# A rotary embedding on one core: another order of loads on SyncE, another branch in the load and store helpers, and a row of small loads

## The chip, the cores and the metric

The kernel runs on one core of one Trainium2 chip. The metric is the device time of one execution in microseconds (us). Three runs of the kernel before gave 316.74 to 316.91 us, with a median of 316.77 us.

Four engines and the transfers matter here. DVE (VectorE) does the arithmetic. ACT (ScalarE) converts small tables. POOL (GpSimd) and SP (SyncE) compute nothing that matters; they issue transfers (DMAs). All transfers run on the same 16 DMA engines, whichever engine has issued them. In the profile the queue of POOL is q0 and that of SP is q1.

## The reference

The input x has the shape (8, 2048, 16, 64): batch, sequence, heads, head dimension. Each position of the sequence has 32 cosines and 32 sines, the same for all batches and heads. All is float32.

```
x1, x2 = x[..., :32], x[..., 32:]
out1 = x1 * cos - x2 * sin
out2 = x1 * sin + x2 * cos
out  = concatenate([out1, out2], axis=-1)
```

x and the output have 67.1 MB each, one batch 8.39 MB.

## The kernel before

A batch is laid over 128 partitions: partition p holds the rows 16p to 16p + 15 of the sequence (J = 16 rows j), each of 16 x 64 elements. In SBUF all is float16. The transfers on POOL convert on their way, float32 to float16 on a load and back on a store.

The tile `buf` has room for five batches; batch b lies in slot b % 5. So batches 5, 6 and 7 go where 0, 1 and 2 lay, and their loads wait for the stores of these.

`rotate(b, j0, j1)` is the arithmetic on the rows j0 to j1 of a batch, three DVE instructions. Line 93 multiplies the two swapped halves by the sines (the first half with a minus sign) into `v`. Line 99 multiplies the batch in place by the cosines. Line 101 adds `v`. Line 93 only reads `buf`; lines 99 and 101 write it.

`load` (line 63) and `store` (line 74) issue on POOL. Each has two branches. With n == 1 it moves one batch, and only the rows that it is told: a store takes j0 and j1, and the load of batch 0 leaves out its first JA = 2 rows. Otherwise it moves n whole batches with one transfer and does not look at j0 or j1. `in_ring` (line 52) ties each of these transfers to the one before it, so that POOL issues them in the order in which the kernel's text names them, and the transfers of POOL follow one another on the DMA engines as on a ring.

The beginning has a path of its own. SP loads the first two rows of batch 0 in float32 into `head` (line 36), then the sines (line 44), then the cosines (line 45). POOL issues load(0), the other 14 rows, and load(1, 3), three batches with one transfer. ACT converts `head` into `buf` (line 105), the sines twice into `sin_h` (lines 109 and 110) and the cosines into `cos_h` (line 111). DVE then rotates rows 0 to 2 of batch 0 and afterwards the other 14.

The order on POOL is: load 0, loads 1 to 3, the first row of batch 0 out, load 4, the other 15 rows of batch 0 out, store 1, store 2, loads 5 and 6, load 7, stores 3 and 4, stores 5 and 6, rows 0 to 9 of batch 7, rows 9 to 14 of batch 7. The last two rows of batch 7 are converted to float32 by ACT into `head` (line 134) and stored by SP (line 135), which is made to wait for the store of rows 0 to 9.

Of the kernel before, what the change touches and what calls it, by code (L numbers as in the profile page):

```python
# [1 line left out]

# [4 lines left out]


@with_exitstack  # L10
def kernel(
    ctx: ExitStack,
    tc: tile.TileContext,
    x: bass.AP,
    cos: bass.AP,
    sin: bass.AP,
    out: bass.AP,
):
    nc = tc.nc
    f16 = mybir.dt.float16  # L20
    f32 = mybir.dt.float32

    B, S, H, D = x.shape
    Dh = D // 2
    P = nc.NUM_PARTITIONS
    J = S // P
    NBUF = 5

    const_pool = ctx.enter_context(tc.tile_pool(name="rope_const", bufs=1))
    io_pool = ctx.enter_context(tc.tile_pool(name="rope_io", bufs=1))  # L30
    tmp_pool = ctx.enter_context(tc.tile_pool(name="rope_tmp", bufs=1))

    JA = 2
    head = const_pool.tile([P, JA, H, D], f32)
    x0 = x[0].rearrange("(p j) h d -> p j (h d)", j=J)
    nc.sync.dma_start(  # L36
        out=head.rearrange("p j h d -> p (j h d)"),
        in_=x0[:, 0:JA, :].rearrange("p j f -> p (j f)"),
    )
    sin_f = const_pool.tile([P, J, Dh], f32)  # L40
    cos_f = const_pool.tile([P, J, Dh], f32)
    cos_h = const_pool.tile([P, J, Dh], f16)
    sin_h = const_pool.tile([P, J, D], f16)
    nc.sync.dma_start(out=sin_f, in_=sin.rearrange("(p j) d -> p j d", j=J))  # L44
    nc.sync.dma_start(out=cos_f, in_=cos.rearrange("(p j) d -> p j d", j=J))


    buf = io_pool.tile([P, NBUF, J, H, D], f16)

    ring = []  # L50

    def in_ring(dma):
        if ring:
            tc.add_manual_dep(
                dma.ins,
                ring[-1].ins.name,
                mybir.DependencyInfo(mybir.DependencyClass.NoSync, mybir.DependencyReason.DATA),
                reason="order of the ring",
            )
        ring.append(dma)  # L60
        return dma

    def load(b, n=1):
        k = b % NBUF
        if n == 1:
            j0 = JA if b == 0 else 0
            dst = buf[:, k, j0:J, :, :].rearrange("p j h d -> p (j h d)")
            src = x[b].rearrange("(p j) h d -> p j (h d)", j=J)[:, j0:J, :].rearrange("p j f -> p (j f)")
        else:
            dst = buf[:, k : k + n, :, :, :].rearrange("p b j h d -> p b (j h d)")  # L70
            src = x[b : b + n].rearrange("b (p j) h d -> p b (j h d)", j=J)
        in_ring(nc.gpsimd.dma_start(out=dst, in_=src))  # L72

    def store(b, n=1, j0=0, j1=J):
        k = b % NBUF
        if n == 1:
            src = buf[:, k, j0:j1, :, :].rearrange("p j h d -> p (j h d)")
            dst = out[b].rearrange("(p j) h d -> p j (h d)", j=J)[:, j0:j1, :].rearrange("p j f -> p (j f)")
        else:
            src = buf[:, k : k + n, :, :, :].rearrange("p b j h d -> p b (j h d)")  # L80
            dst = out[b : b + n].rearrange("b (p j) h d -> p b (j h d)", j=J)
        return in_ring(nc.gpsimd.dma_start(out=dst, in_=src))  # L82

    def rotate(b, j0=0, j1=J):
        v = tmp_pool.tile([P, J, H, D], f16)
        n = j1 - j0
        js = slice(j0, j1)
        xt = buf[:, b % NBUF, js, :, :]
        shape = [P, n, H, 2, Dh]
        sin_b = sin_h[:, js, :].rearrange("p j (e d) -> p j e d", e=2).unsqueeze(2).to_broadcast(shape)  # L90
        cos_b = cos_h[:, js, :].unsqueeze(2).to_broadcast([P, n, 2 * H, Dh])
        xe = xt.rearrange("p j h (e d) -> p j h e d", e=2)
        nc.vector.tensor_mul(  # L93
            out=v[:, js, :, :].rearrange("p j h (e d) -> p j h e d", e=2),
            in0=xe[:, :, :, ::-1, :],
            in1=sin_b,
        )
        xw = xt.rearrange("p j h (e d) -> p j (h e) d", d=Dh)
        nc.vector.tensor_mul(out=xw, in0=xw, in1=cos_b)  # L99
        xa = xt.rearrange("p j h d -> p (j h d)")  # L100
        nc.vector.tensor_add(out=xa, in0=xa, in1=v[:, js, :, :].rearrange("p j h d -> p (j h d)"))  # L101

    load(0)
    load(1, 3)
    nc.scalar.copy(  # L105
        out=buf[:, 0, 0:JA, :, :].rearrange("p j h d -> p (j h d)"),
        in_=head.rearrange("p j h d -> p (j h d)"),
    )
    nc.scalar.copy(out=sin_h[:, :, Dh:D], in_=sin_f)  # L109
    nc.scalar.mul(out=sin_h[:, :, 0:Dh], in_=sin_f, mul=-1.0)  # L110
    nc.scalar.copy(out=cos_h, in_=cos_f)  # L111
    rotate(0, 0, JA)
    store(0, 1, 0, 1)
    load(4)
    rotate(0, JA, J)
    store(0, 1, 1, J)
    rotate(1)
    store(1)
    rotate(2)
    store(2)  # L120
    load(5, 2)
    load(7)
    rotate(3)
    rotate(4)
    store(3, 2)
    rotate(5)
    rotate(6)
    store(5, 2)
    rotate(7)
    gate = store(7, 1, 0, 9)  # L130
    store(7, 1, 9, J - JA)
    last = buf[:, 7 % NBUF, J - JA : J, :, :].rearrange("p j h d -> p (j h d)")
    dst = out[B - 1].rearrange("(p j) h d -> p j (h d)", j=J)[:, J - JA : J, :].rearrange("p j f -> p (j f)")
    nc.scalar.copy(out=head.rearrange("p j h d -> p (j h d)"), in_=last)  # L134
    end = nc.sync.dma_start(out=dst, in_=head.rearrange("p j h d -> p (j h d)"))
    tc.add_manual_dep(
        end.ins,
        gate.ins.name,
        mybir.DependencyInfo(mybir.DependencyClass.Sync, mybir.DependencyReason.DATA),
        reason="the last rows go out behind this part",  # L140
    )


# [1 line left out]
_INS = ['x', 'cos', 'sin']  # L145
_OUTS = [((8, 2048, 16, 64), 'float32')]


# [23 lines left out]
```

## Time and profile before

| what | us |
|---|---|
| median of three runs | 316.77 |
| span of the profiled execution | 315.0 |
| DVE busy | 209.1 (66%) |
| DVE idle until a load had landed | 36.6 |
| DVE idle until the cosines were converted | 16.9 |
| ACT busy | 6.8 |
| POOL busy | 8.1 |

The span is that of one execution under the profiler, from its first to its last instruction; the median is over whole runs without it. The row of the DMA engines in the page's slices gives their mean busy share in tenths for 40 equal parts of the span. The GB/s there are counted on the side of the destination: a load counts in float16, half of what it reads in HBM. The row of HBM counts the bytes in HBM. In the list of issues, the size of a transfer of POOL is that of its float16 side, and the last number is the time from issue to landing. In the table of stretches the columns are: the stretch, its length, the busy time of DVE, ACT and POOL with the number of instructions, the granted clock of TensorE, the share of the DMA engines, and GB/s.

### The profile page before, as it was taken

What the parts mean: (1) busy time and instruction counts of PE and PEld (TensorE: products, weight loads), DVE (VectorE), ACT (ScalarE), POOL (GpSimd) and SP (SyncE); (2) the same over time, 40 slices, a digit from 0 to 9 for tenths busy, and PEclk for the clock granted to TensorE, in tenths of its full rate; (3) what the DMA queues carried; (4) which work ended last, traced back from release to release, by engine and by line L of the source; (5) the groups of instructions that cost most, each with busy time, mean ns of one, the idle gap of its engine ahead of it and who ended that gap; (6) DMA issues with size and microseconds to landing.
All of it is one profiled execution on the core that took longest, in us unless ns stands there. A gap on an engine that the chain in (4) does not pass through costs nothing.

```text
span 315.0 us, 112 instructions
## 1 busy us (share of the span) xinstructions
DVE 209.1 (66%) x27; ACT 6.8 (2%) x6; POOL 8.1 (3%) x17
## 2 busy tenths in 40 slices
DVE  0100999200599999999999970899999999910000
ACT  4100000000000000000000000000000000020000
POOL 2000100000000000010000000000000000010000
DMA  9899999999999899999999999999999999999997
GB/s 278 189 262 204 200 225 241 200 200 241 225 200 317 382 492 407 399 466 466 399 200 241 225 200 200 254 212 333 399 516 416 399 408 516 408 399 458 407 420 313
DMA packets 3089, 101.71 MB, mean 323 GB/s; under 512 B 273, under 2 KB 273, under 8 KB 657
## 3 DMA queue, kind: packets, MB, share of 16 engines
q0 software_dynamic: 2512, 99.09, 98.1%
q1 hardware_dynamic: 576, 2.62, 2.2%
q14 instruction: 1, 0.00, 0.0%
HBM read 67.63 MB, written 67.11 MB: 428 GB/s over the span
## 4 chain that ended last, share of the span: by engine, by line
DVE 66%; another core or an unknown queue 12%; DMA 9%; ACT 1%; issue 0%; SPq 0%; DVEq 0%; ACTq 0%
DVE buf L99 22%; DVE buf L101 22%; DVE v L93 22%; DMA cos_f<-in_cos_dram 9%; ACT head L134 1%; ACT cos_h L111 0%; SPq L44 0%; SPq L36 0%; DVEq L93 0%; ACTq L134 0%
## 5 line engine op out<-in xcount | busy, mean ns | idle before, releaser
L93 DVE TENSOR_TENSOR v<-buf,sin_h 128x16384 f16<-128x16384 f16 (+2 forms) x9 | 69.7, 7744 | 50.1 <-DMA buf<-in_x_dram 36.6
L99 DVE TENSOR_TENSOR buf<-buf,cos_h 128x16384 f16<-128x16384 f16 (+2 forms) x9 | 69.7, 7744 | 17.2 <-ACT cos_h L111 16.9
L101 DVE TENSOR_TENSOR buf<-buf,v 128x16384 f16<-128x16384 f16 (+2 forms) x9 | 69.7, 7744 | 0.3
L82 POOL DMA_DIRECT2D out_dram<-buf x8 | 4.7, 590 | 245.0 <-DVE buf L101 245.0
L134 ACT CAST head<-buf 128x2048 f32<-128x2048 f16 x1 | 1.9, 1897 | 245.4 <-DVE buf L101 245.4
L72 POOL DMA_DIRECT2D buf<-in_x_dram x5 | 3.2, 645 | 24.7 <-DMA out_dram<-buf 23.9
L105 ACT CAST buf<-head 128x2048 f16<-128x2048 f32 x1 | 1.9, 1897 | 3.3 <-DMA head<-in_x_dram 3.3
L105 ACT ACT_TABLE_LOAD x1 | 1.3, 1283 | 0.7 <-PEq L156 0.7
L111 ACT CAST cos_h<-cos_f 128x512 f16<-128x512 f32 x1 | 0.6, 617 | 17.6 <-DMA cos_f<-in_cos_dram 17.6
L109 ACT CAST sin_h<-sin_f 128x512 f16<-128x512 f32 x1 | 0.6, 617 | 4.9 <-DMA sin_f<-in_sin_dram 4.9
L110 ACT ACTIVATE sin_h<-sin_f 128x512 f16<-128x512 f32 x1 | 0.6, 624 | 0.0
L156 POOL MEMSET const-float32-0.0<- 128x1 f32 x1 | 0.1, 98 | 0.2 <-issue 0.2
L156 POOL MEMSET const-bfloat16-1.0<- 128x1 bf16 x1 | 0.1, 101 | 0.0
L156 POOL MEMSET const-float32-1.0<- 128x1 f32 x1 | 0.1, 98 | 0.0
L156 POOL MEMSET const-uint8-127<- 128x1 uint8 x1 | 0.1, 98 | 0.0
## 6 DMA issues: line engine op xcount, KB each, us to landing
buf<-in_x_dram POOLq DMA_DIRECT2D x1, 12288.0 KB, 80.4
buf<-in_x_dram POOLq DMA_DIRECT2D x2, 4096.0 KB, 62.6
buf<-in_x_dram POOLq DMA_DIRECT2D x1, 8192.0 KB, 57.2
out_dram<-buf POOLq DMA_DIRECT2D x1, 7680.0 KB, 63.7
out_dram<-buf POOLq DMA_DIRECT2D x1, 4608.0 KB, 28.6
buf<-in_x_dram POOLq DMA_DIRECT2D x1, 3584.0 KB, 22.6
out_dram<-buf POOLq DMA_DIRECT2D x1, 2560.0 KB, 34.1
head<-in_x_dram SPq DMA_DIRECT2D x1, 1024.0 KB, 4.5
```

The lines of the kernel that those rows point to most:

```text
L72: in_ring(nc.gpsimd.dma_start(out=dst, in_=src))
L82: return in_ring(nc.gpsimd.dma_start(out=dst, in_=src))
L93: nc.vector.tensor_mul(out=v[:, js, :, :].rearrange("p j h (e d) -> p j h e d", e=2), in0=xe[:, :, :, ::-1, :], in1=sin_b,)
L99: nc.vector.tensor_mul(out=xw, in0=xw, in1=cos_b)
L101: nc.vector.tensor_add(out=xa, in0=xa, in1=v[:, js, :, :].rearrange("p j h d -> p (j h d)"))
L105: nc.scalar.copy(out=buf[:, 0, 0:JA, :, :].rearrange("p j h d -> p (j h d)"), in_=head.rearrange("p j h d -> p (j h d)"),)
L109: nc.scalar.copy(out=sin_h[:, :, Dh:D], in_=sin_f)
L110: nc.scalar.mul(out=sin_h[:, :, 0:Dh], in_=sin_f, mul=-1.0)
L111: nc.scalar.copy(out=cos_h, in_=cos_f)
L134: nc.scalar.copy(out=head.rearrange("p j h d -> p (j h d)"), in_=last)
L156: nc = _bacc.Bacc("TRN2", target_bir_lowering=False, num_devices=1)
```

## The change

- On SP the order of the first three loads becomes sines, `head`, cosines.
- In `load` and `store` the test `n == 1` becomes `n == 3`. No call gives 3 any more, so every call takes the other branch: whole batches, without regard to j0, j1 or JA. store(0, 1, 0, 1) and store(0, 1, 1, J) both move the whole batch 0, store(7, 1, 0, 9) and store(7, 1, 9, J - JA) both move the whole batch 7, and load(0) brings all 16 rows, of which ACT writes the first two again from `head`.
- load(1, 3) becomes load(1) ahead of the first store of batch 0 and load(2, 2) behind it.
- On ACT the sines are named before `head`. In the built program the order is sines, sines, cosines, `head`.
- SP issues 14 small loads of 512-byte rows of the sines into a tile `probe` that nobody reads: 3 rows, 4 rows, and so on to 16. The first is made to wait for store(1). They stand on SP between the cosines and the last store. Since they all write the same tile, each waits for the one before it.

```
-    nc.sync.dma_start(
-        out=head.rearrange("p j h d -> p (j h d)"),
-        in_=x0[:, 0:JA, :].rearrange("p j f -> p (j f)"),
-    )
     ...
     nc.sync.dma_start(out=sin_f, in_=sin.rearrange("(p j) d -> p j d", j=J))
+    nc.sync.dma_start(
+        out=head.rearrange("p j h d -> p (j h d)"),
+        in_=x0[:, 0:JA, :].rearrange("p j f -> p (j f)"),
+    )
     nc.sync.dma_start(out=cos_f, in_=cos.rearrange("(p j) d -> p j d", j=J))

     def load(b, n=1):
         k = b % NBUF
-        if n == 1:
+        if n == 3:
     ...
     def store(b, n=1, j0=0, j1=J):
         k = b % NBUF
-        if n == 1:
+        if n == 3:
     ...
     load(0)
-    load(1, 3)
+    load(1)
+    nc.scalar.copy(out=sin_h[:, :, Dh:D], in_=sin_f)
+    nc.scalar.mul(out=sin_h[:, :, 0:Dh], in_=sin_f, mul=-1.0)
     nc.scalar.copy(
         out=buf[:, 0, 0:JA, :, :].rearrange("p j h d -> p (j h d)"),
         in_=head.rearrange("p j h d -> p (j h d)"),
     )
-    nc.scalar.copy(out=sin_h[:, :, Dh:D], in_=sin_f)
-    nc.scalar.mul(out=sin_h[:, :, 0:Dh], in_=sin_f, mul=-1.0)
     nc.scalar.copy(out=cos_h, in_=cos_f)
     rotate(0, 0, JA)
     store(0, 1, 0, 1)
+    load(2, 2)
     load(4)
     rotate(0, JA, J)
     store(0, 1, 1, J)
     rotate(1)
-    store(1)
+    early = store(1)
     ...
     gate = store(7, 1, 0, 9)
     store(7, 1, 9, J - JA)
+    probe = const_pool.tile([16, 128], f32)
+    for n in range(3, 17):
+        d = nc.sync.dma_start(out=probe[0:n, :], in_=sin.rearrange("(p j) d -> p (j d)", j=J)[0:n, 0:128])
+        if n == 3:
+            tc.add_manual_dep(
+                d.ins,
+                early.ins.name,
+                mybir.DependencyInfo(mybir.DependencyClass.Sync, mybir.DependencyReason.DATA),
+                reason="behind this part",
+            )
```

## The prediction

> **What bounds the kernel now.** I read the page's head, slices and queue rows first, to see which resource has no idle time.
>
> ```profile
> span 315.0 us, 112 instructions
> DVE 209.1 (66%) x27; ACT 6.8 (2%) x6; POOL 8.1 (3%) x17
> DMA  9899999999999899999999999999999999999997
> q0 software_dynamic: 2512, 99.09, 98.1%
> q1 hardware_dynamic: 576, 2.62, 2.2%
> HBM read 67.63 MB, written 67.11 MB: 428 GB/s over the span
> ```
>
> DVE is busy for two thirds of the span. The 16 DMA engines show a 9 in all but a few slices, and POOL's queue (q0) alone fills 98.1% of their time. The chain of waits names DVE for 66%, but the transfers are what never stop. The time is therefore a matter of bytes, as long as the ring on POOL always has something queued.
>
> Next, the pace of the ring, from the instructions in order of time around POOL, the stages, and the times to landing.
>
> ```profile
> 140.88 0.71 POOL L72 DMA_DIRECT2D buf<-in_x_dram  x1 [5.35 <-DMA out_dram<-buf]
> 160.14 0.56 POOL L72 DMA_DIRECT2D buf<-in_x_dram  x1 [18.55 <-DMA out_dram<-buf]
> 198.22 8.69 DVE L93 TENSOR_TENSOR v<-buf,sin_h 128x16384 f16<-128x16384 f16 x1 [11.16 <-DMA buf<-in_x_dram]
> 250.84 0.72 POOL L82 DMA_DIRECT2D out_dram<-buf  x1 [62.77 <-DVE buf L101]
> ```
>
> ```profile
> 160.00:198.00 38.00, 26.96 (x4) 0.00 (x0) 1.27 (x2) 1.00 1.02 221
> 217.00:256.00 39.00, 38.86 (x5) 0.00 (x0) 0.72 (x1) 1.00 1.01 434
> ```
>
> ```profile
> buf<-in_x_dram POOLq DMA_DIRECT2D x1, 3584.0 KB, 22.6
> head<-in_x_dram SPq DMA_DIRECT2D x1, 1024.0 KB, 4.5
> out_dram<-head SPq DMA_DIRECT2D x1, 1024.0 KB, 8.4
> sin_f<-in_sin_dram SPq DMA_DIRECT2D x1, 256.0 KB, 10.9
> cos_f<-in_cos_dram SPq DMA_DIRECT2D x1, 256.0 KB, 29.2
> ```
>
> The loads of lines 121 and 122 wait for the stores of batches 1 and 2; they go out 160.14 - 140.88 = 19.3 us apart, so one batch of 8.39 MB takes the ring 19.3 us. Loads cost the same: in 160 to 198 the two batches of line 121 come in (221 GB/s counted in fp16, twice that in HBM), and in 217 to 256 two go out at 434 GB/s. I call 19.3 us a turn. The whole run has (67.63 + 67.11) / 8.39 = 16.06 turns = 310 us; 5 us are left for start and end.
>
> **The change part by part.**
>
> *The branch in load and store.* They now test `n == 3`, and nobody calls them with 3. Every call takes the other branch, which moves whole batches and ignores j0 and j1; the built program's instructions show it (128x16384 rows on POOL). Four things follow:
> - load(0) brings 16 rows instead of 14: 2 rows, 1/8 turn, 2.4 us.
> - The one-row store and the 15-row store of batch 0 both become whole batches. Together they were one turn, now two: +19.3 us.
> - The 9-row and the 5-row store of batch 7 become whole batches: 14/16 of a turn becomes two turns, +1.125 x 19.3 = 21.7 us.
> - Two stores now write the same output, so waits appear: the second store of batch 0 waits for the first, the second of batch 7 for the first, and the last store from `head` for both of batch 7.
>
> Sum of bytes: 18.31 turns instead of 16.06, +43.4 us, all on the bound resource.
>
> *Where the new waits fall.* I lay the ring out in turns. Load 0 landed at 1.25 + 22.6 = 23.9; with two more rows 26.3. Then come load 1 (45.6), store 0 (64.9), loads 2 and 3 (103.5), load 4 (122.8), store 0 again (142.1), stores 1 and 2 (161.4, 180.7), loads 5 and 6 (219.3), load 7 (238.6), stores 3-4 (277.2), stores 5-6 (315.8), store 7 (335.1). Each must be issued before the one ahead of it ends:
> - Store 0: see the head of the kernel, below.
> - rotate(0, 2 to 16) may run its first multiply, but its second writes `buf` rows that store 0 is still reading, so DVE waits until 64.9, some 21 us longer. It ends at 64.9 + 2 x 7.63 = 80.2. The second store 0 goes out then; its place on the ring is at 122.8. POOL queues only that store behind this wait, since load(2,2) and load(4) are ahead of it. Covered by 58 us of loads.
> - Batches 1 to 4 take DVE 3 x 8.72 = 26.2 us each: 106.4, 132.6, 158.8, 185.0, with all their loads in by then. Stores 1, 2 and 3-4 are needed at 142.1, 161.4 and 238.6. Covered.
> - Loads 5-6 wait for store 1 (161.4), needed at 180.7; load 7 waits for store 2 (180.7), needed at 219.3. Covered.
> - Store 5-6 is issued 52.4 us after loads 5-6 land plus 0.3 us, needed 57.9 us after (three turns). That is the same relation as before (198.2, 250.84, some 256), where the DMA share stayed at 9.
> - The second store 7 has no cover. Nothing else is queued, and POOL holds it until the first one has landed. Its price is a turn (counted above) plus the fixed part of a transfer on an idle ring. Bounds: the head load on SP took 4.5 us for 1.05 MB, which move in 2.4 us, so 2.1 fixed; load 0 took 22.6 us with 16.9 for its bytes and 0.8 for sine and cosine rows between them, so 4.9. I take 4.0, nearer to the POOL row, since it is the same queue, less something for its being the first.
>
> The Trainium skill, "DMA: Bandwidth & Descriptors", section "Anatomy of one DMA — SWDGE (gpsimd) path", gives about 2.0 us fixed plus bytes at 436 GB/s. By that the second store 7 would take 21.2 us instead of my 23.3, and the total would be 2.1 us lower; the trace of before never shows this ring idle but at its start, where the row says more.
>
> - The last store from `head` lay beside the 5-row store (8.4 us). Now it follows the second store 7, alone: 4.5 us by the head load, up to 8.4.
>
> *SP's order at the start, and ACT's.* Sine, head, cosine instead of head, sine, cosine. Same bytes. Between 12.05 and 30.8 (cosine's landing) eight rows of cosine per engine took 18.8 us, 2.34 us a row: a small row waits for one ring packet of 64 KB. The order shifts which rows meet the ring: before, three of sine's and all of cosine's; now the end of head and all of cosine. Cosine lands between 27 and 32. ACT now does the cosine cast (0.62) and then the head cast (1.90), which must also wait for load 0 (26.3). DVE starts at 30 to 35, its three short operations take 3.8 us, and store 0 is issued at 34 to 39. The ring needs it at 45.6. With the 4.9 us as the upper bound of the start this is covered, by at least 2 us; without the cover, each us late costs one. Load(2,2) and load(4), behind store 0 on POOL, go out 1 to 2 us after it.
>
> *load(1, 3) as load(1) and load(2, 2).* One more POOL issue, 0.6 us, in POOL's idle time; bytes unchanged. Batch 1 is in at 45.6 instead of 82.4, which brings nothing, as DVE isn't the bound.
>
> *The 14 small loads on SP.* They wait for store 1 (161.4) and, since all write `probe`, each for the one before. By the cosine row one takes at most 29.2 / 8 x 2 = 7.3 us (a row and the completion behind it). 14 of them are done by 264; the only thing behind them on SP is the last store, due at 360. On the engines: q1's row gives 2.2% x 315 x 16 / 576 = 0.19 us per packet. If one engine serves every one of them it loses 14 x 0.19 = 2.7 us; lower bound 0. These rows are smaller than q1's mean, so I take 1.3.
>
> **Sum.** 335.1 + 1.3 (small loads) = 336.4 for the first store 7. + 0.1 + 4.0 + 19.3 = 359.8 for the second. + 4.5 = 364.3 for the last store. + 0.9 (before: landing at 305.72 + 8.4 = 314.1, end at 315.0) = 365.2 us span. The profiled execution had a span of 315.0 against the median of 316.77, 1.8 us around it: 367.0 us. The check by bytes: 310 + 43.4 + 5 + 1.3 + 4.0 + about 2 for the last store = 365.7 span.
> Own range: -1.9 to +0.9 for the fixed part, -1.3 to +1.4 for the small loads, up to +3.9 for the last store, 0.8 either way for the pace (0.05 us a turn): 363 to 374.
>
> **The rivals.**
> 1. *The extra bytes cost nothing (not slower).* If the 428 GB/s were a habit of late issues and not the engines' limit, batch 1's landing 37 us earlier could let the ring run faster. The end would be at 316.8 or under if a turn took (315.0 - 5 - 1.3 - 4.0 - 2) / 18.31 = 16.5 us. For it: single slices of the page show 516 GB/s. Against it: those are bins in which packets begin; over 38 or 39 us both directions stand at 19.3, and the share of the engines is 1.0.
> 2. *The small loads run on few engines and hold the last store.* With all rows of each on one engine, n rows and a completion at 2.4 us a packet and about 1.3 us to start: from 161 on, the loads of 3 to 11 rows take 185 us, until 346. The rest run partly beside the second store 7 and end between 370 and 385; that engine is also some 7 us behind. The last store starts then: 374 to 392 us. It decides from about 14 us a load on (the 199 us to 360, over 14). Against it: one load on its share of the rows takes half of that.
>
> The Trainium skill, same page, section "Why a DMA increments its semaphore by 16 and not by 1", has a load use the largest number of engines up to 16 that divides its slowest dimension. By this rule 3 rows use 3 engines and 13 use 13, one row each, and rival 2 does not come. No run here shows such row counts.
>
> 3. *The ring runs dry at store 0.* If cosine lands at 37 or later, or the descriptors of store 0 take longer beside DVE than 4.9 us, the ring is empty at 45.6; DVE and the store would have to be 3 to 8 us late: 368 to 375 us.
>
> **How the numbers follow.** The forecast 0.87, rival 1 0.01, rival 2 0.07, rival 3 0.05. The predicted time is 367.0. The range 362.5 to 375 takes in the forecast's own bounds and rival 3, and leaves out most of rival 2 and rival 1. A measurement of this kernel tells no change to about 0.2%. Slower 0.98, same 0.01, faster 0.01.
>
> **What would show it.** HBM written about 84.9 MB, read about 68.8; q0's share still above 95%; DVE waiting some 20 us for a store inside batch 0; POOL's last issue at about 336.5 with the DMA slices dipping there once; SP's small loads finished by about 264; the last issue on SP at about 360. I am wrong if the turn isn't 19.3 us, if the last small load is later than 355, or if a slice before 330 shows the engines idle.

## The result, and the profile after

The changed kernel takes 365.34 us (median of 4 runs, 365.19 to 365.37). The kernel before, on the same chip, takes 316.84 us (316.74 to 316.92). The ratio is 1.153, with a 95% interval of 1.152 to 1.155: 48.5 us more. The forecast was 367.0 us with a range of 362.5 to 375. One execution of all those below, 328.29 us of the kernel with the row ranges kept, fell in a slower state of the chip and is not counted.

The head of the page, its slices, its queues and its HBM row, of the changed kernel:

```profile
span 363.6 us, 138 instructions
DVE 209.1 (58%) x27; ACT 6.7 (2%) x6; POOL 8.6 (2%) x18
DMA  9989999999998999899989999999989998998895
q0 software_dynamic: 2528, 117.44, 97.1%
q1 hardware_dynamic: 842, 2.69, 20.0%
HBM read 68.75 MB, written 84.93 MB: 423 GB/s over the span
```

DVE does the same 209.1 us of work. HBM carries 153.68 MB instead of 134.74, at nearly the same rate (423 GB/s against 428). The slices of the DMA engines stay at 8 and 9, with the first real dip at the end. One row has to be read with care: q1 has moved hardly more than before (2.69 MB against 2.62) and yet shows 20.0% of the engines' time instead of 2.2%. That is not work; the last section comes back to it.

The instructions of the changed kernel in order of time, around the places that the prediction named (start, duration, engine, line, operation; in brackets the idle time ahead of it and what ended that):

```profile
33.42 1.23 DVE L92 TENSOR_TENSOR v<-buf,sin_h 128x2048 f16<-128x2048 f16 x1 [33.42 <-ACT buf L106]
37.45 0.54 POOL L81 DMA_DIRECT2D out_dram<-buf  x1 [35.01 <-DVE buf L100]
66.21 7.63 DVE L98 TENSOR_TENSOR buf<-buf,cos_h 128x14336 f16<-128x14336 f16 x1 [21.39 <-DMA out_dram<-buf]
81.80 0.54 POOL L81 DMA_DIRECT2D out_dram<-buf  x1 [42.55 <-DVE buf L100]
162.64 175.84 SPq L134 DMA_DIRECT2D probe<-in_sin_dram  x14
163.19 0.71 POOL L71 DMA_DIRECT2D buf<-in_x_dram  x1 [28.51 <-DMA out_dram<-buf]
182.34 0.56 POOL L71 DMA_DIRECT2D buf<-in_x_dram  x1 [18.44 <-DMA out_dram<-buf]
337.18 0.55 POOL L81 DMA_DIRECT2D out_dram<-buf  x1 [37.14 <-DMA out_dram<-buf]
358.45 0.38 SPq L145 DMA_DIRECT2D out_dram<-head  x1
```

The turn is nearly what it was: 182.34 - 163.19 = 19.2 us between the loads that follow stores 1 and 2, against 19.3. DVE waits 21.39 us inside batch 0 for the store that reads its rows. POOL's last store waits for the one ahead of it and goes out at 337.18; the store from `head` follows at 358.45. The small loads on SP, though, are issued from 162.64 to 338.5, and not done by 264.

### The profile page after: what moved, and what is told of

Same layout as the page of the kernel before. It is cut to its first block, busy times and chain, and to the rows that moved or that the text cites. A ratio compares the mean times of both kernels' runs of the same rounds, so it can differ in the third digit from the quotient of the medians.

```text
span 363.6 us, 138 instructions
## 1 busy us (share of the span) xinstructions
DVE 209.1 (58%) x27; ACT 6.7 (2%) x6; POOL 8.6 (2%) x18
## 3 DMA queue, kind: packets, MB, share of 16 engines
q1 hardware_dynamic: 842, 2.69, 20.0%
HBM read 68.75 MB, written 84.93 MB: 423 GB/s over the span
## 4 chain that ended last, share of the span: by engine, by line
DVE 55%; DMA 16%; issue 11%; another core or an unknown queue 9%; ACT 1%; SPq 0%; POOLq 0%; POOL 0%; DVEq 0%
DVE buf L98 19%; DVE buf L100 19%; DVE v L92 17%; DMA cos_f<-in_cos_dram 8%; DMA out_dram<-buf 8%; ACT buf L106 1%; POOLq L177 0%; POOL out_dram L81 0%; SPq L41 0%; SPq L40 0%; ACT cos_h L110 0%; DVEq L92 0%; DVEq L98 0%
```

## The experiments

The theory is that of the prediction: the ring's bytes, turn by turn, and the places at the end where it is empty make the time. Against it stand the small loads, which ended so much later than forecast, the wait of DVE, and the order of the first loads.

**Without the small loads.**

```
-    probe = const_pool.tile([16, 128], f32)
-    for n in range(3, 17):
-        d = nc.sync.dma_start(out=probe[0:n, :], ...)
...
```

> The changed kernel without its 14 small loads. Theory (the ring's bytes and its two empty places at the end make the time): the small loads cost only their packets on the engines, 0.2 to 0.5 us (nine turns of the ring beside them were 19.34 us each, against 19.31 ahead of them), so 364.8 to 365.2 us against 365.34. Rival (the small loads end at the same time as the second store of batch 7 and hold the last store): 363 us or less.

Measured: 364.41 us (364.32 to 364.51), 0.93 us less. Neither figure was met; it is twice the most of the theory's and less than half the rival's. The last two stores, without the small loads:

```profile
336.92 0.54 POOL L81 DMA_DIRECT2D out_dram<-buf  x1 [36.78 <-DMA out_dram<-buf]
357.98 0.35 SPq L135 DMA_DIRECT2D out_dram<-head  x1
```

And what the last store waits for in the changed kernel, with them:

```profile
SPq L145 <- DMA out_dram<-buf: 19.9, 1, 19.9
```

The last store of POOL goes out at 336.92 instead of 337.18, the last store of SP at 357.98 instead of 358.45, and the end behind it is 0.4 us nearer. The small loads cost 0.9 us in all, and they are not what holds the last store here: that waits for a store of POOL.

**The row ranges kept.** The test is n == 1 again, so that the stores of one row, 15, 9 and 5 rows are what the calls say; the rest of the change stays.

```
-        if n == 3:
+        if n == 1:
```

> The changed kernel with the test n == 1 back in load and store: the row ranges are kept, SP's order, the split load and the 14 small loads stay. If small loads cost next to nothing: 316.8 to 317.4 us. Theory for the small loads (their completion comes in only when the store that is running on POOL's ring ends): they are issued from 141 us, one lands with store 2, eight during the loads, one each with stores 3-4, stores 5-6, the 9-row and the 5-row store, and the last one alone at about 314; the last store starts there instead of at 305.7 beside the ring: about 321 us (320 to 322).

Measured: 319.11, 319.21 and 322.30 us, 1.011 times the kernel before (1.007 to 1.015). Only the slowest of the three, which is the profiled one, lies in the theory's range. So the small loads do hold the last store when the ring ends earlier. The waits of SP's queue, of this kernel (who waited for what: us in total, times, the longest):

```profile
SPq L134 <- DMA probe<-in_sin_dram: 167.8, 13, 38.4
SPq L134 <- DMA out_dram<-buf: 140.9, 1, 140.9
```

```profile
315.40 0.38 SPq L145 DMA_DIRECT2D out_dram<-head  x1
```

The last store starts at 315.40; before, it was 305.72, beside the ring. Single small loads have kept SP waiting for 38.4 us. Not all of the 5.6 us of this execution are theirs, though: the next run shows that 2.9 us were lost before the first small load.

**The row ranges kept, no small loads.** What is left of the change is the order on SP and ACT and the split of the load of batches 1 to 3.

> As the run with the row ranges kept, but without the small loads: only SP's order, ACT's order and the split of the load of batches 1 to 3 are left of the change. Theory (bytes and the end of the ring are those of before): 316.6 to 317.0 us. Rival (batch 1's earlier landing or the order of the first loads moves the end): more than 0.5 us away from 316.8.

Measured: 316.57 us against 316.74, ratio 0.9994 (0.9985 to 1.0003). These parts move nothing that can be measured when the stores are as before. The two kernels are the same up to the small loads, but loads 5 and 6 go out at different times, first with the small loads, then without:

```profile
143.61 0.71 POOL L71 DMA_DIRECT2D buf<-in_x_dram  x1 [25.17 <-DMA out_dram<-buf]
140.69 0.71 POOL L71 DMA_DIRECT2D buf<-in_x_dram  x1 [30.39 <-DMA out_dram<-buf]
```

The first small load is issued at 143.03, so it can't have made these 2.9 us. They belong to the beginning of that one execution: its store 0 goes out at 42.56 instead of 31.82, and for a time between 42.6 and 45.3 not all 16 engines have a packet. In the run without small loads all have one there. What is left for the small loads is about 2.5 us, and that is what the two faster executions show (319.11 and 319.21 against 316.74).

**The branch alone.** The kernel before, with every call on the branch for whole batches.

```
-        if n == 1:
+        if n == 9:
```

> The kernel before with the test n == 9: whole batches for all calls, and one transfer for loads 1 to 3 ahead of the first store of batch 0; no small loads, SP's order of before. Rival (bytes alone decide, the split of the load does nothing): 365 us. Theory: the first store of batch 0 now lies behind load 3 and lands at about 104 instead of 65 us; DVE waits for it until then, stores 1 and 2 come some 5 us late each to an empty ring, so 375 to 379 us.

Measured: 376.0 us (375.8 to 376.3), more than the changed kernel. The rival falls. The waits and the slices of this kernel:

```profile
DVE buf L99 <- DMA out_dram<-buf: 55.2, 1, 55.2
```

```profile
DMA  9998999989999993975999989999999899999795
```

DVE waits 55.2 us inside batch 0 instead of 21.39, because the store of batch 0 now lies behind loads 1 to 3. All later stores move back, and from slice 16 on the ring is empty at times (3, 7, 5). So the split of the load is worth some 11 us once the stores are whole batches. The next run takes this difference by itself.

**One load for batches 1 to 3.** The changed kernel without small loads, with the test n == 9 (with n == 3, the load of three batches would take the branch for one), and with this edit:

```
-    load(1)
+    load(1, 3)
...
-    load(2, 2)
```

> The changed kernel without small loads (364.41 us), with loads 1 to 3 as one transfer ahead of the first store of batch 0 again; whole batches in every call. Theory: it is the split of this load that separates 364.4 from the 376.0 us of the branch alone, since DVE waits for the first store of batch 0 until about 104 instead of 65 us and stores 1 and 2 come late: 375.5 to 376.5 us. Rival (the order of the first loads on SP and ACT has a part in it): under 375.

Measured: 376.18 us (375.93 to 377.33) against 364.41: 11.8 us for the split alone. With one load for the three batches the orders on SP and ACT make no more than 0.2 us (376.18 against the 376.0 of the branch alone).

**The order of the first loads put back.** The changed kernel without small loads, with the order of SP (below) and the names' order on ACT of before.

```
-    nc.sync.dma_start(out=sin_f, ...)
     nc.sync.dma_start(out=head, ...)
+    nc.sync.dma_start(out=sin_f, ...)
     nc.sync.dma_start(out=cos_f, ...)
```

> The changed kernel without small loads (364.41 us), with the order of SP (head, sines, cosines) and the names' order on ACT of before. Theory: cosines land a few us later, the first store of batch 0 is issued at about 42 instead of 37.5, still ahead of the end of load 1 (46): 364.2 to 364.7 us. Rival (the store comes too late for the ring): 366 or more.

Measured: 363.49 us (363.38 to 363.80), 0.9 us less than 364.41. The theory expected no difference. Batch 0 behind its first store, first with the new order, then with the old one:

```profile
66.34 7.63 DVE L98 TENSOR_TENSOR buf<-buf,cos_h 128x14336 f16<-128x14336 f16 x1 [21.79 <-DMA out_dram<-buf]
65.63 7.62 DVE L98 TENSOR_TENSOR buf<-buf,cos_h 128x14336 f16<-128x14336 f16 x1 [15.90 <-DMA out_dram<-buf]
```

Cosine lands at 35.9 instead of 30.7, and store 0 is issued at 42.36 instead of 37.19, yet it lands earlier: DVE goes on at 65.63 instead of 66.34, and POOL's last store goes out at 336.20 instead of 336.92. The new order costs the ring 0.7 us in its first 66 us. With the row ranges kept no such cost was seen (316.57 us against 316.74). Why the same bytes take longer here was not found out.

**Another batch in the place of the second store 7.** `store(4)` sends out again what lies in its slot; it waits for nothing recent.

```
-    store(7, 1, 9, J - JA)
+    store(4)
```

> The changed kernel with store(4) in the place of the second store of batch 7: batch 4 still lies in its slot and goes out a second time, so the bytes are the same and nothing waits for the first store of batch 7 any more but the last store. Theory: the ring doesn't run empty at 336, but the small load of 15 rows now completes only with the end of that store, and the last store, behind it on SP, starts at about 356.7: 363 to 364.5 us. If the small loads don't hold SP: 361 us.

Measured: 363.40 us (363.33 to 363.52), as the theory had it with the last store held by the small loads.

> The same without the 14 small loads. Theory: the last store starts at 337 beside the second store of batch 4; the ring's end is 21.7 us behind the first store of batch 7: 360.5 to 361.5 us, about 3 us under the changed kernel without small loads (364.41). Rival (the empty ring and the last store alone cost nothing): 364.4.

Measured: 361.11 us (360.95 to 361.44). The two empty places at the end, at 337 and ahead of the store from `head`, cost 364.41 - 361.11 = 3.3 us together. The two times come from different chips, and on the one of this run, the one ahead of it and the next two the kernel before took 317.37 us instead of 316.74. Inside the profiles the difference is the same: here the last store goes out behind the first store 7 at

```profile
336.58 0.35 SPq L135 DMA_DIRECT2D out_dram<-head  x1
```

and the span ends 22.6 us later (359.2); without small loads and with the second store 7 it ends 25.8 us behind 336.92 (362.7). The stretches (length, busy us of DVE, ACT and POOL, TensorE's clock, DMA share, GB/s), first of the kernel with the other batch and no small loads, then of the changed kernel:

```profile
330.00:338.00 8.00, 0.00 (x0) 0.00 (x0) 0.00 (x0) 1.00 0.92 393
338.00:358.00 20.00, 0.00 (x0) 0.00 (x0) 0.00 (x0) 1.00 0.99 419
```

```profile
330.00:338.00 8.00, 0.00 (x0) 0.00 (x0) 0.55 (x1) 1.00 0.62 263
338.00:358.00 20.00, 0.00 (x0) 0.00 (x0) 0.00 (x0) 1.00 1.47 420
```

In the changed kernel the share falls to 0.62 where the second store 7 waits for the first. With small loads present, taking this wait away gains less, since the last store then starts at 356.62, behind the small load of 15 rows, and not at 336.58: 2.3 us lie between the two runs.

**One store of batch 0.**

```
-    store(0, 1, 0, 1)
```

> The changed kernel without the first store of batch 0 (the second one brings out the whole batch). Theory (a turn of the ring is a turn of time): 19.3 us less, 346.0 us, and DVE no longer waits inside batch 0. Rival (that wait of DVE, 21.4 us, is what costs, by way of later stores): more than 21 us less, or a gap in the ring that stays.

Measured: 345.77 us (345.58 to 346.88), 19.6 us under the changed kernel: one turn. The chips differ here too; in the profile the last store of POOL goes out 19.5 us earlier (337.18 before):

```profile
317.71 0.54 POOL L81 DMA_DIRECT2D out_dram<-buf  x1 [37.15 <-DMA out_dram<-buf]
```

The wait of DVE inside batch 0 (21.39 us) is gone with it and gains nothing of its own.

**Single stores.** The two stores of a pair of batches become four.

```
-    store(3, 2)
+    store(3)
+    store(4)
...
-    store(5, 2)
+    store(5)
+    store(6)
```

> The changed kernel with stores 3-4 and 5-6 split into four single stores, same order and bytes. Theory on the small loads (completion only at the end of the POOL store that is running): SP's longest wait for one falls from 38.4 to about 19 us, the loads of 12 to 15 rows complete with stores 3, 4, 5 and 6, and the time stays at 364.5 to 365.4. Rival (the waits of 38.4 us go with the number of rows or with all stores together): they stay.

Measured: 365.26 us (365.14 to 365.33), and SP's waits are

```profile
SPq L136 <- DMA probe<-in_sin_dram: 150.7, 13, 19.1
SPq L147 <- DMA out_dram<-buf: 40.4, 1, 40.4
```

The longest wait for a small load is 19.1 us, one turn, where it was 38.4, two turns. The last small load is issued 40 us before the last store, and the time is that of the changed kernel.

**Three rows in each small load.**

```
-        d = nc.sync.dma_start(out=probe[0:n, :], in_=...[0:n, 0:128])
+        d = nc.sync.dma_start(out=probe[0:3, :], in_=...[0:3, 0:128])
```

> The changed kernel with 3 rows in each of the 14 small loads. Theory (what POOL's ring is doing decides how long a small load takes, not its rows): SP's waits are as in the changed kernel, 38.4 us the longest, some 7 us each while loads run, and 365 to 365.5 us. Rival (the waits grow with the rows, 12 to 14 rows being the slow ones): the longest wait falls below 20 us.

Measured: 365.2 us (one run), and

```profile
SPq L134 <- DMA probe<-in_sin_dram: 171.7, 13, 38.4
```

This is the wait of the changed kernel to 0.3 us in 171, with 42 rows instead of 133. The number of rows doesn't matter for these waits.

**The row ranges kept, single stores.** The run that was 2.4 to 5.6 us slower than the kernel before, with the stores of pairs split.

> The kernel with the row ranges kept (test n == 1) and the 14 small loads, but stores 3-4 and 5-6 split into four single stores. Theory: two more small loads complete in the time of these stores, the 16-row one is issued at about 295, the last store starts behind the 9-row store at 305.7 as before: 316.8 to 317.5 us instead of 320.8. Rival (the small loads cost this time in another way): it stays at 320 to 321.

Measured: 317.40 us against 317.35 for the kernel before on this chip, ratio 0.9999 (0.9990 to 1.0009).

```profile
306.38 0.38 SPq L147 DMA_DIRECT2D out_dram<-head  x1
```

The last store starts at 306.38 instead of 315.40, and nothing is left of the difference. So what the small loads cost there, some 2.5 us, was their completion, held up by the two long stores.

## Why the prediction was right, and where it was not

**The bytes.** Written 84.93 MB against the 84.9 forecast, read 68.75 against 68.8. The sum had the first store 7 landed at 336.4, 16 turns and the small loads behind load 0, and the next issue at 336.5; that came at 337.18. A turn taken out took 19.6 us of time with it. This part carries the result. That it came so near is in part luck. DVE went on at 66.21, where the sum had store 0 landed at 64.9, so the beginning took 1.3 us longer than forecast. The 1.3 us for the small loads made up for it: by the end of the first store 7 they had cost 0.3 (337.18 against 336.92 without them).

**The second store 7.** It took from 337.18 to 358.45, 21.3 us with SP's start behind it; the sum had 19.3 + 4.0 = 23.3. The term "fixed part of a transfer on an idle ring" was sized from the first load of the program, and was 2 us too large: about the lower bound (2.1) was measured. The Trainium skill's 2.0 us plus bytes at 436 GB/s ("DMA: Bandwidth & Descriptors", "Anatomy of one DMA — SWDGE (gpsimd) path"), worked out as 21.2 us in the prediction, agrees with the 21.3 us. The first load of a program is no row for this. These 2.0 us too much, 0.7 too little for POOL's issue at 337.18 and 0.2 too much for the end leave a span 1.6 us shorter than forecast (363.6 against 365.2).

**The last store.** From its issue to the end of the span 363.6 - 358.45 = 5.2 us, forecast 4.5 + 0.9.

**The head of the kernel.** DVE began at 33.42 (30 to 35), store 0 went out at 37.45 (34 to 39), the wait inside batch 0 was 21.39 us (some 21). The cover against rival 3 was 45.6 - 39 - 4.9 = 1.7 us and not "at least 2". Rival 3, a dry ring at store 0, did not come in this execution, but its danger was real: in the three kernels that keep the row ranges and split the load, and begin alike, store 0 went out at 29.46, 31.82 and 42.56 us, and the last of them, the first run above that keeps the row ranges, lost 2.9 us there. Why cosine lands so differently from one execution to another was not found out. That the new order costs nothing was wrong by 0.9 us here.

**The split of the load.** "Which brings nothing, as DVE isn't the bound" was the right sum and the wrong sentence. With the row ranges kept it gained nothing (0.9994). But without it the whole batches would have cost 11.8 us more: it is the split that keeps the wait at 21 us, and 21 us are covered by the loads behind, while 51 or 55 are not.

**The small loads.** Their cost was 0.93 us in all against the 1.3 of the sum. The step on their time was wrong: "14 of them are done by 264" took the cosine row, measured while the ring was loading, for all times. The waits of SP's queue in the changed kernel, first between 183 and 246 us, then between 279 and 318:

```profile
SPq L134 <- DMA probe<-in_sin_dram: 55.7, 8, 7.0
```

```profile
SPq L134 <- DMA probe<-in_sin_dram: 76.7, 2, 38.4
```

While loads 5 to 7 ran, eight small loads took 7.0 us each, near the 7.3 that the prediction had as the most; that was 3.65 us for a row and as much for its completion, though the same cosine row gave 2.34 us a row, so the nearness proves nothing about the steps inside. While stores ran, each lasted until the running store of POOL had ended. The last one was issued at 338.17, and that the last store was due only 20 us later is luck: the forecast had not seen these waits. Rival 2 named the right danger, the last store held on SP, for a wrong cause: eight waits of 7.0 us for 4 to 11 rows do not grow with the rows. This agrees with the rule of the Trainium skill that a load runs on the largest number of engines, up to 16, that divides its rows ("DMA: Bandwidth & Descriptors", "Why a DMA increments its semaphore by 16 and not by 1"). The packets fit it too: with the small loads q1 has 842 instead of 576, two for each of the 133 rows. Which engine served each row, these views do not show.

**Rival 1**, that the extra bytes cost nothing, has fallen with the turn: 19.2 us, and 19.6 us for a store taken out.

## What to carry to other kernels

Where the DMA engines show a 9 throughout, count bytes in turns of the ring, and then look for the places where one transfer must wait for another with nothing queued between: those add to it. A wait on an engine that is not the bound is free only as long as what is already queued on the ring outlasts it, so the order of the queue has to be priced together with the wait. A chain of small transfers that ends well ahead of the critical one in one kernel can hold it in another: see what the big queue is doing while the chain runs.

## What had not been expected of the hardware

In these runs a small load on SP's queue completes within 7.0 us while POOL's queue loads, but while that stores, the completion comes only when the running store has ended: 38.4 us beside a store of two batches, 19.1 us beside single ones, with 3 rows as with 14. Why this is so was not shown. The Trainium skill ("DMA: Bandwidth & Descriptors", "Queues, rings and completion order") says that a completion lands only after every earlier write of its DMA engine; that fits in kind. But a wait of 38.4 us, to the end of the whole store, is far longer than the 2.34 us that a row of the cosines waited for a packet of the ring, so this rule alone does not account for it.

The waiting completions are counted as busy time of their queue: q1 shows 20.0% for 2.69 MB, and the DMA share of a stretch rises to 1.47 at an unchanged 420 GB/s. Without small loads q1 shows 1.9%, and with three rows in each, which keep SP waiting as long but have 42 rows instead of 133, 6.3%. A share above 1 is no sign of more work.
